# A hybrid trunk layer on one core: past latents turned in the input phase, constant key rows taken from them, and the turned inverses queued behind attention's first query splits

## The chip, the core and the metric

The kernel runs on one core of a Trainium2 chip. The time is the device time of one execution in microseconds (us); a kernel's time is the median of its runs. Engines are called as the profile calls them: PE (TensorE, matrix products), PEld (its weight loads), DVE (VectorE), ACT (ScalarE), POOL (GpSimd) and SP (SyncE, which only issues DMAs here). Each engine works through its own queue of instructions in order.

## The reference

One layer of a streaming encoder for two groups of requests that share the weights: 1024 prompt tokens and 32 sample tokens, which continue streams with 512 past positions. The kernel handles them as T = 1056 columns of an fp32 activation with 1024 features.

```python
x = LN(alpha * x + Mix(x))      # Mix: attention | S5 | RWKV-7, then one output projection
x = LN(alpha * x + MLP(x))      # squared ReLU, hidden 4096

def mla_mixer(q_lat, kv_lat, k_rope_raw, pos, ckv_past, krope_past, prm):
    q = (rms_norm(q_lat, g_q) @ w_qb)          # 6 heads x (64 nope + 32 rope)
    ckv = rms_norm(kv_lat, g_kv); krope = apply_rope(k_rope_raw, cos, sin)
    ckv_all = concat([ckv_past, ckv]); krope_all = concat([krope_past, krope])
    kv = ckv_all @ w_kvb                       # k_nope | v
    return attend(mla_scores(q_nope, q_rope, k_nope, krope_all), v), ckv, krope
```

For the prompt there is no past and the mask is causal in chunks of 64. RWKV-7 is a linear recurrence with a matrix state per head; the kernel works it in chunks of 64, for which it needs the inverse of a 64 x 64 unit triangular matrix per chunk and head.

## The kernel before, in words

The matrix products of the three large projections are made in fp32 accuracy out of three products of split operands (a high part, hi, and the rest, lo: `split3`, hi on ACT in L49, lo on DVE or POOL in L50; `mm3`, L63, L65, L67). Tokens run in blocks of 384, 384 and 288, contracted features in tiles of 128, eight to a block.

The program has four stages. *Input phase* (to about 306 us): the input projection comes in tiles of 128 output columns (PSUM tag "acc", three buffers; weights wmraw, split to wmhi and wmlo). The first of these tiles that matter here give the low-rank part (`lmix`, a column tile whose mixing with the token before, L238 and L239, feeds `stage_lora`: tanh and sigmoid on ACT as lact, L262 to L264; the gate gt, L297 to L305). Then follow the RWKV tiles of three head pairs (`PAIRS`, 2, 1, 0), the key latent ckv, the rope key (`stage_kr`, L150 to L170), the query latent qn and its products (`stage_q`, L1142: products L1159, evictions L1160, loads of wqa, wqr, ropec and ropes in L1165 to L1177, stores to q_d in L1172) and u (`stage_u`). Latents are normalised with L184 to L191: a square on ACT, a sum over partitions on PE (L185), and L186, L90, L91, L191 on DVE with three small ACT steps between.

*Unit inverses.* Each pair's products for the chunk matrices stand in `rwkv_m` (L718: L726 on PE, evicted at L730; the sample's 32 x 32 block p8 per head, L732 and L733, with the PSUM tag "pti", one buffer; stores to mt_d at L738). `rwkv_inv` (L743) loads all of them as 108 x 2 blocks of 32 x 32 (nn, L755) and inverts them by 31 steps on DVE (L760 product, L761 sum), one after the other. The result y is copied turned (zt, L764, on ACT) and both are stored (zt_d L765, xt_d L766, SP) and loaded again as zb and zc (L777, L778), on which L788 forms the off-diagonal blocks; the inverses go to xt_d (L794) and from there to the scan.

*Attention beside the scan* (to about 840 us): `side_by_side` (L1295) advances two generators, step 0 for attention and S5 and step 1 for the inverses' end and the RWKV scan, with leads of 10 and 14 steps and then 2.5 steps of attention to one of the scan. A scheduler puts the instructions in each engine's order by priorities; `high_priority` lifts a part, and `issue_after` forbids a part to be queued ahead of a given instruction. Step 1 is lifted by 120, and at the first turn must follow the last SP instruction traced so far. Attention itself begins with `attn_past` (L1068: loads of the 512 past latents and rope keys, eight transposes into PSUM, cpast L1079 and kpast L1086), then `attn_setup` (L1089). That makes three key buffers kh, kl and two query buffers qh, ql with a constant row at partition 96 (-1, the rows up to 127 zero), which carries the row maximum through the score product. The constant rows are written into kr (the loaded rope key, whose buffer is also that of the query loads, tag "q") and kpast by memsets (L1102, L1103), split with them, and subtracted from themselves for the zero query rows (L1111). `attn_keys` (L1114) makes the key products sck and splits them, `attn_q` (L1197) loads a head's query (L1202) and splits it, and `attn_max` forms the first scores (sc, PE, L63 to L67). The scan's products begin with pra (L833), on ld loaded from rw.

*Output projection, MLP and the two layer norms* fill the rest, to 1608 us.

## Time and profile before

| what | value |
|---|---|
| runs of the kernel | 1610.67, 1611.26, 1625.8 us; median 1611.26 |
| profiled execution, its own time | 1609.9 us |
| its span | 1608.1 us |
| mean clock granted to PE | 0.965 of full |
| PE busy | 1487.7 us, 93% |
| DVE, ACT, POOL busy | 920.6, 510.6, 415.9 us |

A timeline row has the start and the length in us, the engine, the line of the kernel, the operation, the tile written <- the tiles read, the shape and a count of like instructions that follow each other; in brackets the idle time of the engine ahead of it and what ended that. SPq and ACTq are DMA issues on these engines' queues. A row of waits has the engine and the tile, the instruction that it waited for, the us in total, how often, and the longest. A row of windows has the stretch and its length, the busy us of PE, PEld, DVE, ACT and POOL with the number of instructions, the granted clock, the share of the DMA engines and GB/s. A row of a group has the number of instructions, their busy time and mean in ns, and the idle time before them.

### The profile page before, as it was taken

What the parts mean: (1) busy time and instruction counts of PE and PEld (TensorE: products, weight loads), DVE (VectorE), ACT (ScalarE), POOL (GpSimd) and SP (SyncE); (2) the same over time, 40 slices, a digit from 0 to 9 for tenths busy, and PEclk for the clock granted to TensorE, in tenths of its full rate; (3) what the DMA queues carried; (4) which work ended last, traced back from release to release, by engine and by line L of the source; (5) the groups of instructions that cost most, each with busy time, mean ns of one, the idle gap of its engine ahead of it and who ended that gap; (6) DMA issues with size and microseconds to landing.
All of it is one profiled execution on the core that took longest, in us unless ns stands there. A gap on an engine that the chain in (4) does not pass through costs nothing. (4 is left out here: it accounts for less than half of the span.)

```text
span 1608.1 us, 26358 instructions
## 1 busy us (share of the span) xinstructions
PE 1487.7 (93%) x10855; PEld 1336.1 (83%) x10855; DVE 920.6 (57%) x1676; ACT 510.6 (32%) x991; POOL 415.9 (26%) x394
## 2 busy tenths in 40 slices
PE   7899898578899798888999999999999999999995
PEld 7889786466667566566879999999999999999995
DVE  8476959363566544453865755554454454545457
ACT  5344433314544545542323212222121112221122
POOL 4623663511121101211422221222121112221123
PEclk9999999788999999999999999999999999999998
DMA  5314471437233221233512111111111111111012
GB/s 183 132 59 175 148 191 31 115 87 127 71 86 87 63 75 42 72 98 92 174 56 79 40 40 41 52 53 49 44 43 50 40 40 53 53 40 53 14 41 82
DMA packets 112621, 123.50 MB, mean 77 GB/s; under 512 B 51280, under 2 KB 87812, under 8 KB 112120
## 3 DMA queue, kind: packets, MB, share of 16 engines
q1 hardware_dynamic: 92516, 102.53, 21.8%
q10 hardware_dynamic: 19632, 18.27, 3.8%
q8 instruction: 85, 1.39, 0.4%
q0 software_dynamic: 352, 1.01, 0.2%
q14 instruction: 36, 0.29, 0.1%
HBM read 89.05 MB, written 32.68 MB: 76 GB/s over the span
## 5 line engine op out<-in xcount | busy, mean ns | idle before, releaser
L63 PE MATMUL acc<-xh,uphi 128*128 128x384 f32 (+1 forms) x768 | 249.0, 324 | 0.0
L65 PE MATMUL acc<-xl,uphi 128*128 128x384 f32 (+1 forms) x768 | 248.1, 323 | 0.0
L67 PE MATMUL acc<-xh,uplo 128*128 128x384 f32 (+1 forms) x768 | 247.8, 323 | 0.0
L1538 DVE TENSOR_TENSOR rl<-rl 128x384 f32<-128x384 f32 (+1 forms) x96 | 142.2, 1481 | 176.2 <-ACT rl L1537 174.3
L1566 DVE TENSOR_TENSOR yacc<-yacc,acc 128x384 f32<-128x384 f32 (+2 forms) x344 | 158.9, 508 | 112.1 <-PE acc L67 112.0
L63 PE MATMUL acc<-hh,dnhi 128*128 128x384 f32 (+2 forms) x736 | 209.3, 320 | 0.0
L65 PE MATMUL acc<-hl,dnhi 128*128 128x384 f32 (+2 forms) x736 | 207.2, 320 | 0.0
L67 PE MATMUL acc<-hh,dnlo 128*128 128x384 f32 (+2 forms) x736 | 197.5, 319 | 0.0
L50 POOL TENSOR_TENSOR dnlo<-dnraw,dnhi 128x1024 fp32r<-128x1024 f32 x30 | 72.5, 2417 | 336.8 <-ACT dnhi L49 321.5
L63 PEld LDWEIGHTS acc<-xh,uphi 128*128 128x128 f32 x768 | 144.2, 188 | 0.2 <-ACT xh L49 0.2
L65 PEld LDWEIGHTS acc<-xl,uphi 128*128 128x128 f32 x768 | 144.3, 188 | 0.0
L67 PEld LDWEIGHTS acc<-xh,uplo 128*128 128x128 f32 x768 | 144.3, 188 | 0.0
L50 POOL TENSOR_TENSOR uplo<-upraw,uphi 128x1024 fp32r<-128x1024 f32 x34 | 81.6, 2401 | 238.3 <-ACT uphi L49 238.3
L63 PE MATMUL acc<-xh,wmhi 128*128 128x384 f32 (+3 forms) x384 | 131.9, 344 | 9.3 <-ACT xh L49 8.2
L65 PE MATMUL acc<-xl,wmhi 128*128 128x384 f32 (+3 forms) x384 | 130.2, 339 | 1.6 <-DVE xl L50 1.6
L63 PEld LDWEIGHTS acc<-hh,dnhi 128*128 128x128 f32 x736 | 131.6, 188 | 0.0
L65 PEld LDWEIGHTS acc<-hl,dnhi 128*128 128x128 f32 x736 | 131.5, 188 | 0.0
L67 PE MATMUL acc<-xh,wmlo 128*128 128x384 f32 (+3 forms) x384 | 129.6, 338 | 0.0
L67 PEld LDWEIGHTS acc<-hh,dnlo 128*128 128x128 f32 x736 | 128.9, 188 | 0.0
L49 ACT ACTIVATE dnhi<-dnraw 128x1024 fp32r<-128x1024 f32 x30 | 31.8, 1060 | 298.9 <-PE acc L65 249.2
L49 ACT ACTIVATE hh<-rl 128x384 fp32r<-128x384 f32 (+1 forms) x96 | 47.9, 499 | 148.7 <-DVE rl L1538 148.7
L63 PEld LDWEIGHTS acc<-xh,wmhi 128*128 128x128 f32 (+1 forms) x384 | 73.9, 192 | 12.8 <-ACT xh L49 8.5
(489 smaller groups left out, 2881.2 us busy)
## 6 DMA issues: line engine op xcount, KB each, us to landing
upraw<-in_w_up SPq DMA_DIRECT2D x32, 512.0 KB
dnraw<-in_w_dn SPq DMA_DIRECT2D x30, 512.0 KB
ld<-rw SPq DMA_DIRECT2D x24, 320.0 KB
wmraw<-in_w_m SPq DMA_DIRECT2D x12, 512.0 KB
wo<-in_w_out SPq DMA_DIRECT2D x8, 512.0 KB
z<-in_xa SPq DMA_DIRECT2D x8, 512.0 KB
out_y<-o SPq DMA_DIRECT2D x8, 512.0 KB
xr<-in_xt SPq DMA_DIRECT2D x8, 384.0 KB
```

The lines of the kernel that those rows point to most:

```text
L49: nc.scalar.activation(out=hi, in_=ps, func=AF.Copy)
L50: (lo_eng or nc.vector).tensor_tensor(out=lo, in0=ps, in1=hi.bitcast(F32), op=ALU.subtract)
L63: nc.tensor.matmul(out=outs[i], lhsT=lh, rhs=rhs[i][0], start=start, stop=False)
L65: nc.tensor.matmul(out=outs[i], lhsT=lh, rhs=rhs[i][1], start=False, stop=False)
L67: nc.tensor.matmul(out=outs[i], lhsT=ll, rhs=rhs[i][0], start=False, stop=stop)
L1538: nc.vector.tensor_tensor(out=r[:, :n], in0=r[:, :n], in1=r[:, :n], op=ALU.mult)
L1566: nc.vector.tensor_tensor(out=y, in0=y, in1=ps[i][:, :n], op=ALU.add)
```

## The change

It has six parts.

1. `attn_past` is called in the input phase, right behind the low-rank tile. The past is loaded on ACT's queue into the buffers "mix" of that phase, turned through the PSUM tag "pt", and cpast and kpast stay in a pool that lives on. The constant rows of kpast are written there.
2. `attn_setup` takes the constant rows of the first key buffer and the zero rows of the queries from a broadcast column of kpast (three kinds of instruction: POOL differences for qh, ql and kl, one ACT copy for kh). The splits of kr and kpast cover partitions 64 to 95 alone, and kr needs no constant rows.
3. `rwkv_m` puts the sample products of both heads into one PSUM tile, at partitions 0 to 31 and 64 to 95, and evicts them together behind both large evictions.
4. wqr and ropes are loaded on SP's queue instead of ACT's.
5. In `side_by_side` the first turn of step 0 is lifted by 1500, and the first turn of step 1 must also follow the last ACT instruction traced so far.
6. gt has one buffer instead of two, and the temporary of the rope key's turned output (ko) uses a "mix" buffer; wkv is loaded at the start of `stage_attn`.

```diff
@@ stage_kr, stage_lora
-    ko = g.p1.tile([P, 9, 32], F32, tag="krt", name="ko", bufs=1)
+    ko = g.rawp.tile([P, 9, 32], F32, tag="mix", name="ko", bufs=2)
-        gt = g.lq.tile([P, WSH], F32, tag="o", name="gt", bufs=2)
+        gt = g.lq.tile([P, WSH], F32, tag="o", name="gt", bufs=1)
@@ rwkv_m
+    p8 = g.pti.tile([P, TS], F32, tag="pti", name="pti")
     for h in range(2):
+        nc.tensor.matmul(out=p8[64 * h:64 * h + TS], lhsT=bt[hsl(h), SOFF:WSH], rhs=at[hsl(h), SOFF:WSH], start=True, stop=True)
         nc.scalar.activation(out=nm[:, 0:8, h], in_=ps[h], func=AF.Copy)
-        p8 = g.pti.tile([P, TS], F32, tag="pti", name="pti")[:TS]
-        nc.tensor.matmul(out=p8, lhsT=bt[hsl(h), SOFF:WSH], rhs=at[hsl(h), SOFF:WSH], start=True, stop=True)
-        nc.scalar.activation(out=nm[:TS, 8, h, :TS], in_=p8, func=AF.Copy)
+    for h in range(2):
+        nc.scalar.activation(out=nm[:TS, 8, h, :TS], in_=p8[64 * h:64 * h + TS], func=AF.Copy)
@@ attn_past
-    g.wkv = g.ap0.tile([P, 2, 384], F32, tag="wkv", name="wkv")
-    nc.sync.dma_start(out=g.wkv, in_=g.a["w_kvb"])
-    g.cpast = g.ap0.tile([P, 512], F32, tag="cpast", name="cpast")
-    ct = g.ap.tile([P, 4, P], F32, tag="rec", name="ct", bufs=1)
-    nc.sync.dma_start(out=ct, in_=g.a["ckv0"].rearrange("(t p) c -> p t c", p=P))
-    ps = g.psc.tile([P, 4, P], F32, tag="sc", name="sct")
+    g.cpast = g.keep.tile([P, 512], F32, tag="cpast", name="cpast")
+    ct = g.rawp.tile([P, 4, P], F32, tag="mix", name="ct", bufs=2)
+    nc.scalar.dma_start(out=ct, in_=g.a["ckv0"].rearrange("(t p) c -> p t c", p=P))
+    ps = g.pt.tile([P, 4, P], F32, tag="pt", name="pt")
...
+    nc.gpsimd.memset(g.kpast[96:128], 0.0)
+    nc.gpsimd.memset(g.kpast[96:97], -1.0)
@@ attn_setup
+    cz = bc(g.kpast[96:128, 0:1], [32, 1568])
+    for x in g.q2[0]:
+        nc.gpsimd.tensor_tensor(out=x[96:128], in0=cz[:, 0:T], in1=cz[:, 0:T], op=ALU.subtract)
+    nc.scalar.activation(out=g.kh[0][96:128], in_=cz, func=AF.Copy)
+    nc.gpsimd.tensor_tensor(out=g.kl[0][96:128], in0=cz, in1=cz, op=ALU.subtract)
     nc.sync.dma_start(out=kr[64:96], in_=g.kr_d)
-    for x in (kr, g.kpast):
-        nc.gpsimd.memset(x[96:128], 0.0)
-        nc.gpsimd.memset(x[96:97], -1.0)
     for x, o, c, n in ((g.kpast, TP, 0, 512), (kr, 0, 0, TP), (kr, 1536, TP, TS)):
-        split3(g, x[64:128, c:c + n], g.kh[0][64:128, o:o + n], g.kl[0][64:128, o:o + n])
+        split3(g, x[64:96, c:c + n], g.kh[0][64:96, o:o + n], g.kl[0][64:96, o:o + n])
...
-        for x in g.q2[i] if i < 2 else ():
-            nc.gpsimd.tensor_tensor(out=x[96:128], in0=kr[96:128, 0:T], in1=kr[96:128, 0:T], op=ALU.subtract)
+        for x in g.q2[i] if i == 1 else ():
+            nc.gpsimd.tensor_tensor(out=x[96:128], in0=cz[:, 0:T], in1=cz[:, 0:T], op=ALU.subtract)
@@ stage_q
-            nc.scalar.dma_start(out=wr[:, k, j, x:x + 32 * n] ...
+            nc.sync.dma_start(out=wr[:, k, j, x:x + 32 * n] ...
-        nc.scalar.dma_start(out=sn[32 * h:32 * h + 32], in_=g.a["rope"][32:64])
+        nc.sync.dma_start(out=sn[32 * h:32 * h + 32], in_=g.a["rope"][32:64])
@@ side_by_side
-            step(0, a)
+            with g.tc.high_priority(FRONT) if k == 0 else nullcontext():
+                step(0, a)
             n -= 1
         if not done[1]:
-            with g.tc.high_priority(PRIO), g.tc.issue_after(last_traced(g, mybir.EngineType.SP)) if k == 0 else nullcontext():
+            with ExitStack() as s:
+                s.enter_context(g.tc.high_priority(PRIO))
+                for e in (mybir.EngineType.SP, mybir.EngineType.Activation) if k == 0 else ():
+                    s.enter_context(g.tc.issue_after(last_traced(g, e)))
                 step(1, b)
@@ stage_attn
-    attn_past(g)
-    yield
+    g.wkv = g.ap0.tile([P, 2, 384], F32, tag="wkv", name="wkv")
+    nc.sync.dma_start(out=g.wkv, in_=g.a["w_kvb"])
     attn_setup(g)
@@ tile_trunk
                 g.lmix = mixed(g, raw_in(g, 3, 9, w=w0), 9)
+                attn_past(g)
```

The scheduler moves more than these lines say. Line numbers in the changed kernel are one higher from L735 on and three higher behind the set-up. The first place is ACT's queue in the input phase, between the evictions of the third and the fourth column tile. Before:

```order
28 L226 ACTIVATE raw<-acc 128x384
29 L49 ACTIVATE wmhi<-wmraw 128x1024
30 L227 ACTIVATE raw<-acc 128x256
31 L228 ACTIVATE raw<-acc 128x32
32 L262 ACT_TABLE_LOAD
33 L262 ACTIVATE lact<-mix 32x1058
34 L263 ACTIVATE lact<-mix 32x1058
35 L264 ACT_TABLE_LOAD
36 L264 ACTIVATE lact<-mix 64x1058
```

In the change:

```order
28 L1074 DMA ct<-in_ckv 128x4x128
29 L226 ACTIVATE raw<-acc 128x384
30 L1078 ACTIVATE cpast<-pt 128x512
31 L1080 DMA kt<-in_kr 128x4x32
32 L262 ACT_TABLE_LOAD
33 L262 ACTIVATE lact<-mix 32x1058
34 L263 ACTIVATE lact<-mix 32x1058
35 L264 ACT_TABLE_LOAD
36 L264 ACTIVATE lact<-mix 64x1058
37 L49 ACTIVATE wmhi<-wmraw 128x1024
38 L227 ACTIVATE raw<-acc 128x256
39 L228 ACTIVATE raw<-acc 128x32
```

The past's loads and first eviction came in, and the weight split (L49) and two evictions (L227, L228) moved from ahead of the low-rank activations to behind them.

The second place is DVE's queue at the norm of the query latents (L186, L90, L91, L191), which shares the queue with the steps of the inverse (L760, L761; L761, L762 in the change). The last extent of a step's product falls from 512 in its middle to 62 at its end. Before, about step 16:

```order
301 L186 TENSOR_SCALAR pt<-pt 128x384
302 L760 TENSOR_TENSOR tmp<-y,nn 108x512
303 L761 TENSOR_TENSOR y<-y,tmp 108x2x16x16
304 L760 TENSOR_TENSOR tmp<-y,nn 108x510
305 L90 SCALAR_TENSOR_TENSOR rms<-rms,pt 128x384
306 L761 TENSOR_TENSOR y<-y,tmp 108x2x17x15
307 L186 TENSOR_SCALAR pt<-pt 128x384
308 L91 SCALAR_TENSOR_TENSOR rms<-rms 128x384
309 L760 TENSOR_TENSOR tmp<-y,nn 108x504
310 L191 SCALAR_TENSOR_TENSOR qn<-qn,vec,rms 128x384 x2
```

In the change, about step 29:

```order
329 L186 TENSOR_SCALAR pt<-pt 128x384
330 L762 TENSOR_TENSOR y<-y,tmp 108x2x29x3
331 L90 SCALAR_TENSOR_TENSOR rms<-rms,pt 128x384
332 L761 TENSOR_TENSOR tmp<-y,nn 108x120
333 L91 SCALAR_TENSOR_TENSOR rms<-rms 128x384
334 L762 TENSOR_TENSOR y<-y,tmp 108x2x30x2
335 L191 SCALAR_TENSOR_TENSOR qn<-qn,vec,rms 128x384 x2
336 L761 TENSOR_TENSOR tmp<-y,nn 108x62
337 L90 SCALAR_TENSOR_TENSOR rms<-rms,pt 128x384
338 L762 TENSOR_TENSOR y<-y,tmp 108x2x31
339 L91 SCALAR_TENSOR_TENSOR rms<-rms 128x384
```

The norm of the first query block moved from the chain's middle to its last steps (its own first L186 stands behind the 27th product), and the chain's first steps now follow directly on the products of the last head pair, ahead of the key latent's norm.

The third place is ACT's queue about the turned inverse, zt. Before:

```order
248 L1172 DMA q_d<-qnope 64x1056 x2
249 L1160 ACTIVATE qropeb<-scq 128x288
250 L1160 ACTIVATE qropeb<-scq 128x384
251 L764 ACTIVATE zt<-y 108x1024
252 L1160 ACTIVATE qnope<-scq 128x384 x3
253 L148 ACTIVATE ut<-acc 128x8x48 x2
```

In the change:

```order
263 L49 ACTIVATE kh<-sck 64x512
264 L49 ACTIVATE kh<-sck 64x32
265 L49 ACTIVATE qh<-q 96x544
266 L49 ACTIVATE qh<-q 96x512
267 L765 ACTIVATE zt<-y 108x1024
268 L49 ACTIVATE qh<-q 96x512
```

It moved from among the evictions of the query products to behind the splits of head 0's query.

12 lines of the change are left out of this document (6 added, 6 removed).

## The prediction

> **What bounds the kernel now.** I read the page first, then stretches of the span, then what TensorE (PE) waited for, then the rows around each wait.
>
> ```profile
> span 1608.1 us, 26358 instructions
> PE 1487.7 (93%) x10855; PEld 1336.1 (83%) x10855; DVE 920.6 (57%) x1676; ACT 510.6 (32%) x991; POOL 415.9 (26%) x394
> ```
>
> PE is busy for 93% of the span, so time can only come out of its gaps, which lie in the first half. Stretches, with the busy time of PE, PEld, DVE, ACT and POOL, the granted clock, the DMA share and GB/s:
>
> ```profile
> 80.00:170.00 90.00, 90.00 (x542) 80.08 (x540) 62.65 (x164) 39.26 (x65) 29.03 (x47) 0.98 0.31 108
> ...
> 280.00:290.00 10.00, 0.51 (x3) 0.05 (x1) 8.02 (x10) 1.64 (x1) 9.46 (x10) 0.69 0.30 76
> ...
> 306.00:322.00 16.00, 6.24 (x20) 2.62 (x18) 8.79 (x11) 7.48 (x15) 15.21 (x12) 0.76 0.44 129
> 322.00:330.00 8.00, 6.00 (x20) 4.60 (x21) 5.94 (x13) 1.23 (x3) 1.72 (x2) 0.62 0.95 230
> ```
>
> From 80 to 170 us PE has no gap at all: work that comes late before 80 is passed on, not absorbed. At 280 to 290 it does half a microsecond of work, and at 306 to 322 six of sixteen. The waits of PE name the causes:
>
> ```profile
> PE scq L1159 <- ACT qnope L1160: 10.2, 1, 10.2
> PE sck L1119 <- DVE kl L50: 9.8, 4, 4.9
> ...
> PE pti L732 <- ACT kk L733: 5.6, 3, 3.3
> ...
> PE scq L1159 <- DVE qn L191: 3.3, 3, 1.6
> ```
>
> The largest one, in a row of ACT and one of PE:
>
> ```profile
> 288.36 1.94 ACT L764 ACTIVATE zt<-y 108x1024 f32<-108x1024 f32 x1 [12.17 <-DVE y L761]
> ...
> 290.73 4.10 PE L1159 MATMUL scq<-qn,wqa 128*128 128x288 f32 x8 [10.23 <-ACT qnope L1160]
> ```
>
> ACT runs its queue in order. The turned inverse (zt) stands between two evictions of query products and waits 12.17 us for the inverse's last step on DVE, at 288; PE finds no free PSUM and stands for 10.23.
>
> **The change, part by part.**
>
> *zt behind head 0's query splits.* The 10.23 us wait goes, and the evictions behind zt run at PE's pace. zt itself is not needed there: its store (L765, row below) went out only at 318.24. That is a gain of 10.2, if nothing else holds the query products.
>
> *The inverse chain and the query norm.* Something else does. The 31 steps of the chain (L760, L761) share DVE with the norms of the key and query latents.
>
> ```profile
> 209.60 0.31 ACTq L738 DMA_DIRECT2D mt_d<-kk  x1
> 215.22 0.34 ACTq L755 DMA_DIRECT2D nn<-mt_d  x1
> 218.62 2.44 POOL L162 TENSOR_TENSOR krt<-krc,ropek 32x1056 f32<-32x1056 f32 x1
> ...
> 227.07 0.56 DVE L90 SCALAR_TENSOR_TENSOR rms<-rms,pt 128x384 f32<-128x384 f32 x1 [6.37 <-DMA ropec<-in_rope]
> 227.54 0.22 DVE L760 TENSOR_TENSOR tmp<-y,nn 108x62 f32<-108x62 f32 x1
> 251.80 0.56 DVE L186 TENSOR_SCALAR pt<-pt 128x384 f32<-128x384 f32 x1
> 257.58 1.56 PE L1159 MATMUL scq<-qn,wqr 128*128 128x384 f32 x4 [1.31 <-DVE qn L191]
> ...
> 269.90 2.67 POOL L1181 TENSOR_TENSOR qrope<-qrope,ropec 128x1056 f32<-128x1056 f32 x1 [25.53 <-ACT qrope L1160]
> ...
> 270.32 2.62 DVE L761 TENSOR_TENSOR y<-y,tmp 108x350 f32<-108x350 f32 x1
> ```
>
> Before, the chain stood behind a key norm (L90) that waited 6.37 us on ACT, where eight loads of wqr were being issued (the row names the ropec load, the last event by time); it began at 227.54, and the first query norm (L186, 251.80) stood in its middle, 5.8 us ahead of the first query product. In the new order nothing but the loads of nn stands ahead of the chain, and the first query norm stands behind its 27th step. With wqr and ropes on SP, ACT is free of that blockade.
>
> When does the chain begin? Its last input was issued at 215.22, 5.6 us after the last store of the blocks (209.60) that it reads. The pair of sample products spares some of the 5.6 us of pti waits on that path. Bounds: 210 (all of the pti wait off, and 0.5 us to land) and 221 (nothing spared, landing another 5.6 us). I take 214. How long to step 27? The group rows of the two lines:
>
> ```profile
> L761 DVE TENSOR_TENSOR y<-y,tmp 108x62 f32<-108x62 f32 (+15 forms) x31 | 26.9, 868 | 0.8
> L760 DVE TENSOR_TENSOR tmp<-y,nn 108x62 f32<-108x62 f32 (+15 forms) x31 | 22.6, 728 | 0.7
> ```
>
> These 49.5 us hold eight operations like that of 270.32: it took 2.62 beside a POOL product of 2.67, where its neighbours of the same width take about 0.5, some 2.1 us extra each. So the chain's own work is 49.5 - 8 x 2.1 = 33, of which 30 precede the query norm. To it come three key norms (four operations each, like that of 251.80, about 0.5: 6), one mix (twice a norm's operation by its width: 1.3), and six POOL products of 2.4 us like that of 218.62, which now run beside the chain (rope of the key, weight splits, a mix): 6 x 2.1 = 13. Sum 50.3; with the small gaps between steps I use 52, which puts L186 at 266, and with the 4.7 that the norm takes with its interleaved steps, the first query product starts near 270.7 instead of 257.58: **+13.1** (bounds +7 and +22: 210 with one hold fewer at the low end, 221 with one more at the high end). PE arrives earlier than that (by its row it stood free 1.31 ahead of 257.58, at 256.3; at most 3.3 of lateness from below come to it), so it waits there.
>
> [...]
>
> *Query products.*
>
> ```profile
> 294.38 0.63 PE L63 MATMUL acc<-xh,wmhi 128*128 128x384 f32 x1
> ...
> 306.17 0.29 PE L67 MATMUL acc<-xh,wmlo 128*128 128x288 f32 x1
> ...
> 308.02 1.13 PE L1119 MATMUL sck<-ckv,wkv 128*128 128x512 f32 x2 [0.68 <-ACT cpast L1079]
> ```
>
> From 257.58 to the last input block at 294.4 were 36.8 us; less 10.2, and less the rest of the waits on qn (3.3 less the first 1.3, 1.9), leaves 24.7. New: 270.7 + 24.7 = 295.4. The block itself (12.0) and a pair of latent products that now stands inside it (1.1) give 308.5, against 306.4: **+2.1**.
>
> *Attention's set-up.*
>
> ```profile
> 310.56 2.92 POOL L1111 TENSOR_TENSOR ql<-kr 32x1056 fp32r<-32x1056 f32 x1
> ...
> 315.91 1.94 POOL L1111 TENSOR_TENSOR ql<-kr 32x1056 fp32r<-32x1056 f32 x1
> ...
> 317.88 0.32 SPq L1202 DMA_DIRECT2D q<-q_d  x1
> 318.24 0.40 SPq L765 DMA_DIRECT2D zt_d<-zt  x1
> ...
> 322.36 0.45 PE L63 MATMUL sc<-kh,qh 128*128 128x128 f32 x1 [3.33 <-POOL kl L1109]
> ```
>
> From the last input product (306.17 + 0.29) to the first score was 15.9 us. The query load waited for POOL's last constant row at 317.85 to give back kr's buffer. Now kr is read by the splits alone, so the load is free earlier, and turning the past (eight transposes, two evictions, the wait of 0.68 above) is gone from here. Of sck's waits on DVE's splits (9.8 above) the first pair's moves into the last block, ahead of its end. What remains is POOL: the constant rows still stand behind a memset that waited for PE; qh and ql of head 0 (1.94 + 2.92) and kl, 1568 wide, by the same rate 2.92 to 4.3: 7.9 to 9.2 after the last product. I take 9 (bounds 8, and 16 if the set-up stays as it was): **-6.9**. First score at 317.5 instead of 322.36: **-4.8**.
>
> *Early phase.* The eight transposes move to 30 to 50 us.
>
> ```profile
> 37.53 1.06 ACT L49 ACTIVATE wmhi<-wmraw 128x1024 fp32r<-128x1024 f32 x1 [2.62 <-PE acc L65]
> ...
> 45.16 1.09 ACT L262 ACTIVATE lact<-mix 32x1058 f32<-32x1058 f32 x1 [4.91 <-DVE mix L239]
> ...
> 50.31 0.44 PE L63 MATMUL acc<-xh,wmhi 128*128 128x384 f32 x1 [1.11 <-ACT raw L225]
> ```
>
> There the next weight split and two evictions, on ACT from 37.53 before, now stand behind the three lact operations and a table load, the first of which waited until 45.16 for DVE. The eviction behind that group let PE go at 50.31; less its own half microsecond the group ends at 49.8, and with 1.06 and two short evictions (0.6) those are done at 51.5. PE's block of 50.31 needs that split and POOL's behind it (some 2.4), so it starts about 4 later; I estimate that one of them is caught up: 3.3 late at 80 us, and no gap until 170 to absorb it. It costs nothing of its own, because PE arrives at the query products with 8 us to spare; without that cover it costs 3.3 (bounds 0 and 4.2). The p8 pair saves up to 5.6, hidden by the same wait; without that wait it counts.
>
> *Rest.* Three rows on the two smaller edits: who waited for the gate's store, the last load of the inverse's blocks, and the products on them.
>
> ```profile
>   POOL gt L298: 1.6, 1
> ...
> L778 SPq DMA_DIRECT2D zb<-xt_d x4: 427/488/488, 326.1 to 327.7; - x4
> ...
> L788 PE MATMUL pti<-zb,n x128: 191/191/212, 337.9 to 340.5; 32*32 32x32 f32 x128
> ```
>
> One gt buffer instead of two makes POOL wait for that store twice instead of once, at 120 to 135, hidden while PE has blocks in hand (bounds 0 and 2 x 1.6). zt now follows head 0's query splits: its store comes about 1.5 us after the first score instead of 4.1 ahead, 5.6 later. The loads behind it were issued by 327.7; if they land within the 5.6 that the chain's loads had at most, 4.6 us are left to 337.9. So 1 us may be lost: I take 0, bounds 0 and 3. Behind 340 us the order on PE is nearly the same, so the gain there passes to the end.
>
> Sum: +13.1 - 10.2 - 1.9 + 1.1 - 6.9 = -4.8; a colder array after shorter gaps is priced next.
>
> ```profile
> 326.55 0.63 PE L63 MATMUL sc<-kh,qh 128*128 128x512 f32 x1
> ...
> 328.42 0.39 PE L67 MATMUL sc<-kh,ql 128*128 128x512 f32 x1
> ```
>
> After the long gap a 512-wide score took 0.63, then 0.39. A gap of 9 instead of 16 us may start warmer; I take 0.3 off (bounds 0 and 2). [...]
>
> So -5.1: the span goes from 1608.1 to 1603.0, the profiled run (1609.9) to 1604.8. The median shown, 1611.26, stands 1.4 above that run: **1606.2**.
>
> **The rivals.**
>
> *B, the waits simply go.* The chain is through before PE arrives: it starts at 210, and POOL holds it less. Then 10.2, 1.9, the pti waits of 5.6 and the set-up's 6.9 all count, less 1.1 moved and the early 3.3: -20.2, so 1591. For it: 13 us of lead over 227.54. Against it: the query norm's place behind step 27 and the POOL products.
>
> *C, the query norm decides.* The chain starts at 221, with two more holds (4.2): L186 at 277.2, first query product 281.9, first score 328.7, +6.3, and the store of the inverse 2 more: 1620. If the set-up also stays at 16, 1627. Each us of delay counts in full; slower than before begins at a chain start of 219. For it: one row of 5.6 us for such a store-and-load. Against it: DVE waits for nothing else there.
>
> *D, nothing comes through.* The first score comes earlier, but the scan behind it is bound by the inverse and its stores, which do not: 1611. For it:
>
> ```profile
> PE pra L833 <- DMA ld<-rw: 6.7, 2, 6.5
> ```
>
> This wait of 6.5 us at 366 hangs on SP's queue behind the inverse's stores. Against it: those follow L788, which moves with the scores.
>
> **How the numbers follow.** Forecast 0.48 (own range 1598 to 1613), B 0.22, C 0.20, D 0.10. About 1% (16 us) is what a measurement of this kernel can tell from no change. Faster by more (below 1595): most of B and a tail of the forecast, 0.23. Slower by more (above 1627): the far half of C and mishaps of the early phase, 0.14. Within: 0.63. The range 1590.5 to 1622.5 leaves out somewhat less than half of B and the far part of C.
>
> **What would show it.** Right: no wait of L1159 on qnope; instead one wait of 6 to 12 us of the first L1159 on qn L191, near 262 to 271; the chain's first step at 212 to 219 with several of its early steps at 2.4 us; first score 8 to 11 us after the last input product; PE's fourth block 3 to 4 us late at 50 us. Wrong: a first query product before 262 (then B), or after 278 (C), or a PE gap after 330 us that was not there.

## The result, and the profile after

The changed kernel takes 1620.99 us, the median of 20 runs (1615.93 to 1630.71); the kernel before, beside it, 1612.62 (20 runs, 1608.4 to 1625.8). The ratio is 1.0051, with a 95% interval of 1.0033 to 1.0069: 8 us slower, where 5 us faster was forecast. The time lies just inside the top of the range (1622.5), and within what rival C gave (1620 to 1627).

The first lines of the page after. PE is busy nearly as long (1489.2 us against 1487.7), so the loss is in its gaps:

```profile
span 1616.0 us, 26354 instructions
PE 1489.2 (92%) x10855; PEld 1338.5 (83%) x10855; DVE 914.4 (57%) x1676; ACT 513.6 (32%) x992; POOL 416.1 (26%) x393
```

The waits of PE after (total, times, longest). The 10.2 us of L1159 on qnope are gone, as forecast. Two waits of nearly that size stand at the top in their place, and neither is in the prediction: the key norm's sum of squares (L185), and a product of the scan (L841).

```profile
PE pt L185 <- ACT rms L184: 10.0, 2, 6.2
PE sck L1122 <- DVE kl L50: 9.8, 5, 2.4
PE prt L841 <- ACT wu L884: 8.7, 1, 8.7
...
PE acc L63 <- ACT raw L228: 4.3, 1, 4.3
```

The stretches shown before, and one more, 212 to 220 us (busy time of PE, PEld, DVE, ACT, POOL; clock; DMA share; GB/s):

```profile
80.00:170.00 90.00, 89.88 (x549) 79.69 (x550) 65.89 (x168) 43.23 (x73) 31.75 (x49) 1.00 0.37 133
212.00:220.00 8.00, 1.47 (x6) 1.06 (x7) 2.11 (x8) 1.23 (x4) 1.96 (x2) 0.71 0.76 198
280.00:290.00 10.00, 10.00 (x36) 6.65 (x35) 0.78 (x2) 3.80 (x9) 5.84 (x3) 1.00 0.09 19
306.00:322.00 16.00, 8.80 (x45) 6.89 (x43) 8.07 (x11) 8.47 (x16) 13.16 (x11) 0.76 0.46 134
322.00:330.00 8.00, 5.55 (x18) 4.20 (x18) 4.96 (x10) 2.41 (x2) 1.40 (x1) 0.62 0.65 185
```

The kernel before at 212 to 220:

```profile
212.00:220.00 8.00, 8.00 (x46) 7.74 (x45) 0.00 (x0) 2.57 (x5) 7.92 (x6) 1.00 1.00 252
```

At 280 to 290 PE is now full instead of empty. At 212 to 220 it is the other way round: 1.47 us of work instead of 8.00. The gap has moved 70 us ahead.

The places that the prediction spoke of, on the timeline after (start, length, engine, line):

```profile
217.53 0.23 DVE L761 TENSOR_TENSOR tmp<-y,nn 108x62 f32<-108x62 f32 x1 [19.16 <-DMA rw<-mix]
...
267.98 0.56 DVE L186 TENSOR_SCALAR pt<-pt 128x384 f32<-128x384 f32 x1
...
272.72 1.00 PE L1162 MATMUL scq<-qn,wqr 128*128 128x384 f32 x2 [3.25 <-DVE qn L191]
...
298.54 0.44 PE L63 MATMUL acc<-xh,wmhi 128*128 128x384 f32 x1 [0.29 <-ACT ut L148]
...
311.83 0.29 PE L67 MATMUL acc<-xh,wmlo 128*128 128x288 f32 x1
...
322.62 0.44 PE L63 MATMUL sc<-kh,qh 128*128 128x128 f32 x1 [3.48 <-ACT qh L49]
```

Matched product by product, PE is 13 us later than before at 225 to 245 us and 15 later at the first query product; it is 0.3 later at the first score (322.62 against 322.36), 4 to 5 later at 330 to 345, within 2.5 us either way from 360 to 570, 6 to 8 later behind the gap at 584, and 8.6 later from 840 to the last products. So in this execution the wait that went and the waits that came cancel by the first score, and the loss that lasts is taken at 584. Whether that place is the cause is a question for the runs.

### The profile page after: what moved, and what is told of

It is laid out like the page before. It is cut to its first block, busy times and chain, and to the rows that moved or that the text cites. A ratio compares the mean times of both kernels' runs of the same rounds, so it can differ in the third digit from the quotient of the medians.

```text
span 1616.0 us, 26354 instructions
## 1 busy us (share of the span) xinstructions
PE 1489.2 (92%) x10855; PEld 1338.5 (83%) x10855; DVE 914.4 (57%) x1676; ACT 513.6 (32%) x992; POOL 416.1 (26%) x393
## 5 line engine op out<-in xcount | busy, mean ns | idle before, releaser
L65 PE MATMUL acc<-xl,wmhi 128*128 128x384 f32 (+3 forms) x384 | 133.7, 348 | 1.6 <-DVE xl L50 1.6
L49 ACT ACTIVATE dnhi<-dnraw 128x1024 fp32r<-128x1024 f32 x30 | 31.8, 1060 | 301.2 <-PE acc L65 249.2
L49 ACT ACTIVATE hh<-rl 128x384 fp32r<-128x384 f32 (+1 forms) x96 | 47.9, 499 | 148.8 <-DVE rl L1545 148.8
```

The costliest lines, as they stand in the source:

```text
L49: nc.scalar.activation(out=hi, in_=ps, func=AF.Copy)
L65: nc.tensor.matmul(out=outs[i], lhsT=lh, rhs=rhs[i][1], start=False, stop=False)
```

## Where PE stands at 212 to 238

Rows of ACT, DVE and PE in the changed kernel, in order of time (mt_d and rw are stores, "ACTq" their issue):

```profile
204.28 2.19 ACTq L739 DMA_DIRECT2D mt_d<-kk  x4
206.51 2.06 ACTq L336 DMA_DIRECT2D rw<-mix  x1
...
210.91 0.34 ACTq L336 DMA_DIRECT2D rw<-mix  x1
211.29 0.44 ACTq L337 DMA_DIRECT2D rw<-mix  x1
...
219.04 0.52 ACT L184 ACTIVATE rms<-ckv 128x384 f32<-128x384 f32 x1 [6.77 <-DMA rw<-mix]
219.62 1.65 PE L185 MATMUL pt<-rms,ones 128*128 128x384 f32 x2 [6.21 <-ACT rms L184]
...
223.69 0.55 DVE L186 TENSOR_SCALAR pt<-pt 128x384 f32<-128x384 f32 x1
231.76 0.55 DVE L90 SCALAR_TENSOR_TENSOR rms<-rms,pt 128x384 f32<-128x384 f32 x1
234.44 0.55 DVE L91 SCALAR_TENSOR_TENSOR rms<-rms 128x384 f32<-128x384 f32 x1
235.34 0.61 DVE L191 SCALAR_TENSOR_TENSOR ckv<-ckv,vec,rms 128x384 f32<-128x384 f32 x1
235.99 0.52 ACT L184 ACTIVATE rms<-ckv 128x384 f32<-128x384 f32 x1 [8.65 <-DVE ckv L191]
236.56 1.65 PE L185 MATMUL pt<-rms,ones 128*128 128x384 f32 x2 [3.77 <-ACT rms L184]
```

The same two instructions in the kernel before, and the square in the change without the pair (run f1 below):

```profile
217.72 0.53 ACT L184 ACTIVATE rms<-ckv 128x384 f32<-128x384 f32 x1 [4.05 <-DMA rw<-mix]
219.29 0.81 PE L185 MATMUL pt<-rms,ones 128*128 128x384 f32 x2
...
212.28 0.52 ACT L184 ACTIVATE rms<-ckv 128x384 f32<-128x384 f32 x1 [3.29 <-DMA rw<-mix]
```

The norm's scratch tile (rms, L180) shares two buffers with mix. The first one comes free when the last mix but one is stored. With the pair of sample products all four stores of a head pair's blocks (mt_d) and a load of them (210.49 on ACT's queue) stand ahead of that store; its issue ends at 211.73, and the buffer is back 7.3 us later. Without the pair (f1) three of the four stores stand ahead of it, its issue ends at 208.47, and the buffer is back 3.8 us later. Before, the square of the first key block waited for a mix store too (until 217.72), so against that kernel the buffer is only 1.3 us late, and L185 starts at the same time. But PE then had input products to work on until 219.29 and waited for nothing. In the new order L185 stands ahead of that work: PE has done 870 input products (counted from the start) ahead of it instead of 912. It is not the pair that brings it forward. With the past's move alone (e7) and in the change without the pair (e6, f1) it stands behind 844, with the pair and the loads alone (e8) behind 900. So the past's move takes PE's work away from ahead of L185, and the pair makes the buffer late.

The second wait is the inverse's. The other buffer holds the last mix, which is stored only at 236.05, so the second block needs the first one's buffer. The four norm operations of the first block on DVE, half a microsecond each, take from 223.69 to 235.95, because they now stand among the chain's first steps; so the buffer is back at 235.95. From 205 us to the first query product PE waits 15.3 us in four places (2.06 on krc, 6.21, 3.77, 3.25), before 4.7 (1.06, 2.28, 1.31). And between 205 and 250 us the array runs 17 us at half clock, before 3.4.

## The experiments

Each group of kernels ran beside the kernel before on one chip, and each ratio is to that. The theories: **G**, the place of S5's activation (L683) on ACT costs the time at 584; **I**, the input phase costs it, ahead of the first score; **N**, the query norm's place behind the inverse's 27th step; **Q**, zt's store ahead of head 1's query load on SP; **M**, the mix buffer that comes back late; **V**, the key norm among the inverse's steps; **P**, the pair costs only where it meets the past's move; **K**, the granted clock: time at half clock gives a lead back.

### The activation at 584

After, the activation's table load waits 9.07 us for its input, and the scan's eviction wu (L884) stands behind it:

```profile
584.07 1.28 ACT L683 ACT_TABLE_LOAD   x1 [9.07 <-DMA zt<-z_d]
585.37 1.98 ACT L683 ACTIVATE zt<-zt 128x2128 f32<-128x2128 f32 x1
587.36 1.28 ACT L76 ACT_TABLE_LOAD   x1
588.65 0.87 ACT L884 ACTIVATE wu<-prw 128x512 f32<-128x512 f32 x2
...
589.31 1.12 PE L841 MATMUL prt<-ident,ld 128*128 128x128 f32 x4 [8.69 <-ACT wu L884]
```

Before, four other operations of ACT had gone ahead of it, and it waited 3.35:

```profile
584.76 1.28 ACT L683 ACT_TABLE_LOAD   x1 [3.35 <-DMA zt<-z_d]
```

No line of the diff touches it; the scheduler moved it. The edit holds it back in the changed kernel (e1) and in the one before (e2):

```diff
-    log_exp_table(g, [nc.scalar.activation(out=zt, in_=zt, func=AF.Gelu_apprx_tanh)], False)
     yield
+    with g.tc.issue_after(last_traced(g, mybir.EngineType.Activation)):
+        log_exp_table(g, [nc.scalar.activation(out=zt, in_=zt, func=AF.Gelu_apprx_tanh)], False)
     yield
```

> The changed kernel with one addition: S5's gelu (L683, which needs two table loads and sixteen loads of z) may not be queued on ScalarE ahead of the instruction that was traced last at its step, which puts it behind the evictions of the next scan block. Theory G (the gelu): the whole loss of the changed kernel is the wait of 8.7 us that TensorE has at 589 us, because the gelu stands ahead of wu, ptk, po and r and waits 9.07 us for its loads. Then that wait is gone, and the span falls from 1616.0 to 1605 to 1609. Rival I (the input phase): the loss is made before 340 us (query products 15 us later than before, second scores 4.2 us later) and only shows at the end; then the span stays at 1613 or above.

Measured: 1617.86 us, 1.0031 [1.0016, 1.0045].

> The kernel before with the same addition. Its own gelu holds r<-prt, and TensorE waits 3.8 us for that at 590. Theory G: that wait goes, and the span falls from 1608.1 to 1604 to 1606. Rival I says nothing of it; a rival within G is that the gelu's readers (s5g) then wait instead: no change, 1607 to 1609.

Measured: 1607.5 us, 0.9974 [0.996, 0.9988]. The activation's place costs both kernels about the same, 0.2 to 0.26%. With it held in both, the change is still 0.57% slower (1.0031 against 0.9974). G falls as the cause, although the profile after shows its whole loss there. All kernels below have this edit, except where said.

### The parts of the change, one by one

zt behind head 0's query splits alone, on the kernel before, the activation not held (e3) and held (e5):

```diff
-            with g.tc.high_priority(PRIO), g.tc.issue_after(last_traced(g, mybir.EngineType.SP)) if k == 0 else nullcontext():
+            with ExitStack() as s:
+                s.enter_context(g.tc.high_priority(PRIO))
+                for e in (mybir.EngineType.SP, mybir.EngineType.Activation) if k == 0 else ():
+                    s.enter_context(g.tc.issue_after(last_traced(g, e)))
                 step(1, b)
```

> The kernel before with one part of the change: the first turn of the inverses' step must also follow ScalarE's last traced instruction (no lift of 1500, the past in its old place). The 10.23 us wait of the query products on zt goes, and the query norm stays in the middle of the chain. Rival I and the prediction's own view: first score 8 to 11 us earlier than 322.4, and most of it reaches the end: span 1598 to 1601. Theory G alone: what is won before 340 us is lost again on the way to 570, since all engines meet again at the scan's first load, and only the gelu's place matters (here a few evictions earlier than before): 1605 to 1611.

Measured: 1612.06 us, 1.0008 [0.9983, 1.0033]. The first score starts at 311.64 instead of 322.36, a lead of 10.7. At 400 us 5 of them are left, at 550 none. (The profile is of this kernel's slowest execution, 1626.31.)

> The kernel before with two edits: zt queued behind head 0's query splits (as in the third run) and the gelu held (as in the second, which came to 0.9974 of before, 1607.5 us). In the third run's profile the first score came 12 us earlier than before, the lead was down to 5 at 380 and 0 at 560, and the gelu's other place then cost 8. Theory I (the input phase decides): with the gelu out of the way some of the lead stays, 0.990 to 0.995 of before. Theory K (the clock): PE is granted half clock in spells of 3.4 us or multiples, and denser work brings more of them later, so that the lead is given back: 0.996 to 1.000.

Measured: 1601.79 us, 0.9945 [0.9925, 0.9965], against 0.9974 with the activation held alone. The first query product is at 255.28 and the first score at 307.76. Of 13.5 us of lead (321.28 in e2) some 5 reach the end. This part does what it says.

The past's move, the constant rows and the smaller buffers alone (e7), and the pair of sample products with the loads on SP alone (e8):

> The kernel before with the gelu held and, of the change, only the early past with its constant rows and the smaller buffers (no pair, loads of wqr and ropes on ScalarE, zt where it was, no lift). Theory I: it costs the early wait of 4.3 us at 51 us, which is made good by 100, and the set-up is shorter: 0.993 to 0.998. If the early past itself is what loses (ScalarE's queue at 40 us, or the set-up bound by something else), 1.000 to 1.004.

Measured: 1614.91 us, 1.0013 [0.999, 1.0035].

> The kernel before with the gelu held and, of the change, only the pair of sample products and the loads of wqr and ropes on SyncE. The chain then goes ahead of the key norms, the first query norm behind step 20 or so, and zt stands earlier among the evictions. Theory I: the key norms and the query products wait for the chain, 5 to 9 us, and zt's wait is not removed: 1.000 to 1.005. Theory K: 0.996 to 0.999, as without them.

Measured: 1605.98 us, 0.9964 [0.9943, 0.9986]. Against 0.9974 the past's move costs some 0.4%, and the pair and the loads gain nothing that can be told. In e7 the first query product comes at 264.47, 8.2 us later than in e2 (256.30), without any pair. In e8 PE waits 5.74 us at L185, as in the changed kernel, and yet starts the query products at 256.47; its first score, at 310.56, is 10.7 us earlier than in e2, and no gain from it can be told in the time. All of the change but the past's move and the constant rows (h2):

> The kernel before with the pair of sample products, the loads on SP, zt behind the query splits, and the activation of S5 held back: the change without the past's move and the constant rows. Theory P (TensorE is made late at 200 to 240 us only where the pair meets the past's move): first query product at 256 to 258 us, query products through by 284, first score at 306 to 311, ratio 0.990 to 0.995. If the pair alone makes it late: first query product at 265 or later, ratio 0.999 to 1.003. If the time is set by half-clock spells (theory K), as with zt's move alone: first score as early, and the ratio no better than 0.998.

Measured: 1603.93 us, 0.9956 [0.993, 0.9981]; first query product at 261.4, first score at 315.4. PE does wait there for the key norm, once, 5.53 us, so theory P's "only where they meet" is wrong for the wait. The ratio is that of zt's move alone (e5), though the first score is 7.7 us later.

The whole change without the pair, the activation held (e6) and not held (f1):

```diff
-    p8 = g.pti.tile([P, TS], F32, tag="pti", name="pti")
     for h in range(2):
-        nc.tensor.matmul(out=p8[64 * h:64 * h + TS], lhsT=bt[hsl(h), SOFF:WSH], rhs=at[hsl(h), SOFF:WSH], start=True, stop=True)
         nc.scalar.activation(out=nm[:, 0:8, h], in_=ps[h], func=AF.Copy)
-    for h in range(2):
-        nc.scalar.activation(out=nm[:TS, 8, h, :TS], in_=p8[64 * h:64 * h + TS], func=AF.Copy)
+        p8 = g.pti.tile([P, TS], F32, tag="pti", name="pti")[:TS]
+        nc.tensor.matmul(out=p8, lhsT=bt[hsl(h), SOFF:WSH], rhs=at[hsl(h), SOFF:WSH], start=True, stop=True)
+        nc.scalar.activation(out=nm[:TS, 8, h, :TS], in_=p8, func=AF.Copy)
```

> The changed kernel with the gelu held (1.0031 of before) and without the pair of sample products (each head's again by itself). The order on VectorE is then near that of before: the first query norm stands behind step 20 of the chain, not behind step 27. Theory I: the pair is what lets the chain go first; the first query product comes at 258 to 264 instead of 272.7, and of the 9 us by which the changed kernel lies behind the one before, both with the gelu held, 5 or more go: 0.994 to 0.999. Theory K: the order here does not matter, 1.001 to 1.005.

Measured: 1599.63 us, 0.9935 [0.9913, 0.9958], the fastest of all, faster than both kernels. PE waits for no square at L185; the query products start 8 us earlier than in the changed kernel:

```profile
214.37 0.81 PE L185 MATMUL pt<-rms,ones 128*128 128x384 f32 x2
...
264.57 0.81 PE L1162 MATMUL scq<-qn,wqr 128*128 128x384 f32 x2
...
315.56 0.44 PE L63 MATMUL sc<-kh,qh 128*128 128x128 f32 x1 [3.44 <-ACT qh L49]
```

> The whole change without the pair of sample products, and with the activation of S5 where the scheduler puts it. With that activation held back the same kernel took 0.9935 of the time before, and the whole change 1.0031. If the pair is what turns the change into a loss (theory N, below), this run is faster than before too: 0.994 to 0.997, with the first query product at 263 to 266 us as in the run with the activation held. If the loss needs the activation's place (theory G), it is at 1.000 or above.

Measured: 1608.67 us, 0.998 [0.9959, 1.0002].

```profile
212.86 0.91 PE L185 MATMUL pt<-rms,ones 128*128 128x384 f32 x2 [1.57 <-ACT rms L184]
...
236.47 0.90 PE L208 MATMUL pt<-ident,ckv 128*128 128x128 f32 x3 [6.06 <-DVE rms L90]
```

The first wait is nearly gone; the second has another form, since PE still meets a key norm that stands among the inverse's steps. So the one part that was priced as a hidden saving turns the change into a loss: without it 0.998 instead of 1.0051, with the activation held 0.9935 instead of 1.0031. It does so only beside the past's move: with zt's move and the activation held, the ratio is 0.9945 with neither (e5), 0.9956 with the pair (h2), 0.9935 with the past's move (e6) and 1.0031 with both (e1). The loads on SP are in all of these but e5, and the lift goes with the past's move. So for the time theory P holds.

### What of the pair costs it

The inverse behind the query norm (e4): the chain is held behind the norm's last operation on DVE.

```diff
+    yield
     for s in range(31):
...
         stage_q_in(g)
+        with tc.issue_after(last_traced(g, DVE)):
+            next(inv)
```

> The changed kernel with the gelu held (as in the first of these runs) and with the 31 steps of the inverse put behind the query norms on VectorE. The first query product comes as soon as its latents are there, at 255 to 260 instead of 272.7; the first score at 306 to 312 instead of 322.6. If earlier scores reach the end (rival I turned round), the span is 8 to 14 below that of the first run, 1592 to 1599. If the scan's start sets the pace after 370 us (theory G alone), it is within 3 us of the first run.

Measured: 1621.32 us, 1.0051 [1.0038, 1.0065]. It only moved the wait: the key splits on DVE now stand behind the chain.

```profile
PE sck L1124 <- DVE kl L50: 31.4, 5, 25.7
```

The query norm ahead of the 21st step (f2): the same hold, with the `yield` at `s == 20`.

> The whole change with the activation of S5 held back, and with the query norm ahead of the 21st step of the inverse on VectorE, where the kernel without the pair has it. Theory N says that the pair costs its time through the place of the query norm alone: first query product at 258 to 266 us instead of 273.8, first score at 314 to 318 instead of 323.8, ratio 0.993 to 0.997. Theory Q says that the pair costs it at 330 us, through SP's queue, where zt's store stands ahead of head 1's query load: first score earlier as well, but 4 us or more are given back at 330, ratio 0.998 to 1.001. If neither holds (the time is set behind 340 us, by the clock), 1.003 as without this edit.

Measured: 1615.08 us, 1.0007 [0.9983, 1.0032].

```profile
219.87 1.65 PE L185 MATMUL pt<-rms,ones 128*128 128x384 f32 x2 [6.46 <-ACT rms L184]
236.84 1.65 PE L185 MATMUL pt<-rms,ones 128*128 128x384 f32 x2 [4.30 <-ACT rms L184]
271.58 2.01 PE L1165 MATMUL scq<-qn,wqr 128*128 128x384 f32 x4 [2.36 <-DVE qn L191]
```

The first query product came only 1.9 us earlier than in e1 (273.43). N falls: the norm was late because PE was, and PE was late at L185.

zt's store from ScalarE (f3: `nc.scalar.dma_start(out=g.zt_d, in_=zt)`), and with the norm early as well (f4):

> The whole change with the activation of S5 held back, and zt's store issued from ScalarE, right behind zt, so that head 1's query load does not stand behind it on SP. Theory Q: the 4.2 us at 330 us go, ratio 0.999 to 1.001 against 1.0031 without this edit. Theory N: first query product still at 273 to 274, ratio 1.001 to 1.003, since only those 4 us can go.

Measured: 1611.92 us, 0.9995 [0.9971, 1.0019]. The ratio is theory Q's, the rows are not:

```profile
320.75 0.52 SPq L768 DMA_DIRECT2D xt_d<-y  x1
327.25 0.31 SPq L1206 DMA_DIRECT2D q<-q_d  x1
...
332.61 1.18 ACT L49 ACTIVATE qh<-q 96x512 fp32r<-96x512 f32 x2 [5.64 <-DMA q<-q_d]
```

Head 1's query load is no longer behind the store, and still goes out only 6 us after the row ahead of it; ACT waits 5.64 us for it (6.88 in the changed kernel, 6.77 in the one before). The wait is not the store's, and why this kernel is faster stays open.

> Both edits together, on the whole change with the activation of S5 held back. If N and Q each hold a part of the pair's cost, this is the sum: first query product at 258 to 266 us, no loss at 330, ratio 0.990 to 0.994, at or below the kernel without the pair (0.9935). If N alone counts, it is as with the norm early alone; if neither, 1.003.

Measured: 1610.74 us, 0.9991 [0.9967, 1.0014]: no better than one of them.

The first block of each norm in a buffer of its own (g1; g4 is the change as it is with this line alone, the activation not held):

```diff
-        w = g.rawp.tile([P, 2, 512], F32, tag="mix", name="rms", bufs=2)
+        w = (g.rawp if b else g.p1).tile([P, 2, 512], F32, tag="mix" if b else "kk", name="rms", bufs=2 if b else 3)
```

> The whole change with the activation of S5 held back, and the first block of each norm in a buffer of another pool (kk, free since the head pairs' stores), so that its square does not wait for the mix buffer. Theory M (the mix buffer and what follows from it cost TensorE its place): the wait of 6.2 at 219 us goes, that at 236 shrinks or goes, first query product at 262 to 268 us instead of 273.8, last input product at 302 to 307, ratio 0.994 to 0.998. Theory V (the key norm's place among the inverse's steps on VectorE): the wait at 219 goes but the one at 236 grows by as much, first query product within 2 us of 273.8, ratio 1.002 to 1.004. Theory K (the time is set by half-clock spells and not by these waits): 1.003.

Measured: 1609.56 us, 0.9974 [0.9952, 0.9996].

> The whole change as it is, with the first block of each norm in the other buffer and nothing else. If theory M holds, it is faster than before or equal: 0.996 to 1.000, against 1.0051 for the change. If not, 1.004 to 1.006.

Measured: 1614.42 us, 1.0007 [0.999, 1.0023], against 1.0051 without that line. Rows of g1:

```profile
199.87 0.81 PE L185 MATMUL pt<-rms,ones 128*128 128x384 f32 x2
...
222.09 1.65 PE L185 MATMUL pt<-rms,ones 128*128 128x384 f32 x2 [8.54 <-ACT rms L184]
...
268.68 0.81 PE L1163 MATMUL scq<-qn,wqr 128*128 128x384 f32 x2
```

The first block no longer waits, but the second takes the mix buffer in its place and waits for the same store; the first query product still comes 5 us earlier and does not wait for its norm. The gain was forecast, the shape of the waits was not.

The inverse behind the key norm alone (g2: the hold of e4, placed behind `stage_kv_in`), and with the buffer (g3):

> The whole change with the activation of S5 held back, and the first step of the inverse held behind the last block of the key norm on VectorE. Theory V: the wait at 236 us goes (the one at 219 stays), the inverse starts near 230 and ends near 290, first query product at 262 to 268, ratio 0.996 to 0.999. Theory M: the wait at 219 stays and carries on, first query product at 268 to 273, ratio 1.000 to 1.003. Theory K: 1.003.

Measured: 1613.09 us, 0.9998 [0.9976, 1.0019]. The wait at 236 goes, that at 224 stays (6.58); first query product at 269.6.

> Both edits. Theories M and V each take half of the ten us: no wait of L185 over 2 us, first query product at 256 to 262 us, first score at 308 to 314, ratio 0.991 to 0.995. Theory K: first score as early, but the ratio no better than 0.998, because the half-clock time between 300 and 800 us grows.

Measured: 1612.4 us, 0.9988 [0.9956, 1.002]. The first query product is at 261.12, the first score at 317.50, later than expected (308 to 314), and the time is no better than with the buffer alone. Here theory K came nearest.

The stores of the blocks from SP, so that the mix store is issued earlier on ACT (h1):

```diff
-            nc.scalar.dma_start(out=dst[c], in_=nmv[64 * c + 32 * f:64 * c + 32 * f + 32, :, 32 * f:32 * f + 32])
+            nc.sync.dma_start(out=dst[c], in_=nmv[64 * c + 32 * f:64 * c + 32 * f + 32, :, 32 * f:32 * f + 32])
```

> The whole change with the activation of S5 held back, and the stores of the inverse's blocks (mt_d) issued from SP instead of ScalarE. Theory M (the mix buffer comes back late because its store is queued behind those four stores): the wait of the key norm's square is at most 2 us and ends by 214 instead of 219, TensorE is at most 6 us late at 240 us, first query product at 262 to 267, first score at 313 to 317, ratio 0.994 to 0.998. If the buffer is late for another reason (the transfers themselves are slow there, with the loads of wqr beside them), the wait stays at 5 us or more, and the ratio at 1.002 to 1.004.

Measured: 1606.46 us, 0.9958 [0.9938, 0.9978], 0.73% less than e1.

```profile
216.50 0.52 ACT L184 ACTIVATE rms<-ckv 128x384 f32<-128x384 f32 x1 [5.77 <-DMA rw<-mix]
217.08 0.91 PE L185 MATMUL pt<-rms,ones 128*128 128x384 f32 x2 [2.17 <-ACT rms L184]
...
231.13 1.65 PE L185 MATMUL pt<-rms,ones 128*128 128x384 f32 x2 [3.88 <-ACT rms L184]
...
267.94 0.91 PE L1163 MATMUL scq<-qn,wqr 128*128 128x384 f32 x2
```

The buffer comes back at 216.5 instead of 219, PE's first wait falls from 6.2 to 2.2, and the first query product is 5.5 us ahead of e1's, without a wait for its norm. That speaks for theory M, though the mix store still needs 6.4 us to land. The edit does not change the buffer alone: the scheduler now puts L185 behind 847 input products instead of 870, and the query norm's last operation behind 23 of the chain's products instead of 30; in g1 and g4 it stands behind 22. So these runs don't part the late buffer from the order on DVE.

## Why the prediction was wrong

- **The chain.** Start forecast at 214 (bounds 210 and 221), measured 217.53; the query norm's first step (L186) at 266, measured 267.98. Right within 4 us, and the norm did wait behind the chain's 27th product, 267.62. Six early steps held beside POOL's products were forecast; seven steps took 2.22 to 2.75 us where the chain's other operations of 224 to 512 columns took 0.39 to 0.69, and each of the seven began within 1.2 us of the start of a POOL operation of 2.4 to 3.5 us (219.99 to 255.00). The 0.5 us to land in the lower bound was the author's estimate, and no run shows it: the last load of nn was issued at 210.49, and the first step on it began 7.0 us later.
- **The first query product.** Forecast 270.7, measured 272.72. The number was right and its cause only in part: PE was to arrive at 256 to 260 and wait 11 us and more; it arrived at 269.5 and waited 3.25. That the number came within 2 us is luck. The forecast "6 to 12 us" of waiting is the mark that failed.
- **The failed step** is PE's arrival at the query products: "PE arrives earlier than that", at 256.3 with "at most 3.3 of lateness from below", and with it "it costs nothing of its own, because PE arrives at the query products with 8 us to spare". The waits for the key norm ahead of that place were put at nothing. They measured 10.0 us (6.21 and 3.77), beside 2.06 on krc and 17 us at half clock instead of 3.4, and PE arrived 10 to 13 us later than forecast. The spare time was PE's own work ahead of L185, and the past's move took L185 forward into it: alone, with the smaller buffers, it makes the first query product 8.2 us later (e7 against e2). Of the pair it was written that it "saves up to 5.6, hidden"; what it does to ACT's queue (the block of four stores ahead of the store that frees a buffer) was not looked at, and it adds 8.9 (273.43 in e1 against 264.57 in e6). Runs f1, e6, g4 and h1 take the pair or its consequence away, and each brings the ratio from 1.0031 or 1.0051 down to 1.0007 or less. But f2, f3, f4 and g2, which leave the first wait, also come to between 0.9991 and 1.0007; by the intervals only e6 is clear of all of them. "DVE waits for nothing else there" was true and missed the point: the key norm waits for DVE, and PE for the key norm.
- **Query products and last block.** 24.7 and 13.1 forecast, 25.8 (272.72 to 298.54) and 13.6 (to 312.12) measured. **Set-up**: 9 forecast, 10.5 measured (312.12 to 322.62), since ACT's query split waited 1.27 for its load. The four misses, 2.0, 1.1, 0.5 and 1.5, add up to 5.1: the whole forecast lead of 4.8 at the first score, and 0.3 more. The 0.3 taken off for a warmer start was the author's estimate as well, and no run shows it: the granted clock is 0.50 from 314.4 to 328.1 us in both traces.
- **Early phase.** The wait came, 4.3 us at 51, but the sizes were off: PE was 5.5 us late at 60 (about 4 forecast) and 0.9 at 80 (3.3 forecast). It caught up at 74 to 80, where the array ran at full clock (1.00) and in the kernel before at 0.59, and by 100 nothing was left.
- **zt's store.** Forecast 0 (bounds 0 and 3). The first product on the inverse's blocks comes 19.5 us after the first score (342.2) instead of 15.5: 4 us, outside the bounds, and made up by 380.
- **"Behind 340 us the order on PE is nearly the same, so the gain there passes to the end"** is the second step that failed. Of the 13 us between the forecast change of the span (-5.1) and the measured one (+7.9), 5.1 arise by the first score and the rest behind it, with a PE gap of 8.69 us at 584 to 589, where the kernel before had one of 3.78; the prediction names such a gap as a sign of being wrong. e3 lost 11 us of lead by 550, and in e5 5 of 13.5 us reached the end. The order on PE is the same there, but the order on ACT is not (the activation at 584), and PE's clock is not. The pair shows it with the activation held: e1 is 7.9 us behind e6 at the first score and 19 from 410 on. From 320 to 360 us e1's granted clock is 0.63 and e6's 0.88, so some 30 and 10 us at half clock; by an estimate that gives 10 of the 11 us in these two executions. Other executions need not fall so.
- **Rival C** gave the time (1620) from another mechanism: its chain start (221) and its first query product (281.9) did not come.

What stays open: not all of the 8 us has a place. Of each microsecond gained at the first score only a part shows at the end, differently from kernel to kernel; the edits of f2, f3 and g1 gain 0.2 to 0.6% each and do not add up (f4, g3). Why the two late waits cost time beside the past's move, and a wait of the same size at L185 in e8 and h2 none that can be told, is not shown.

## What to carry to other kernels

A part that shortens one engine's queue by a few evictions can reorder the DMAs on that queue; ask which of them frees a buffer, who waits for that buffer, and whether PE still has work ahead of the instruction that needs it (here 870 input products ahead of it instead of the 912 of the kernel before, and a buffer back 7.3 us behind its store's issue instead of the 3.8 of f1). Spare time on PE belonged to an order here, not to an interval: it can't be taken over into a new order without reading where the waiting instruction now stands. A part that costs nothing alone can cost beside another one, so take each out of the whole as well as putting it in alone. When the largest new wait in one profile explains the whole loss, hold it back in both kernels before believing it.

## What the hardware showed that was not expected

PE's granted clock in the 20 traces is full or half, nothing between, in stretches that are multiples of 3.41 us. In the kernel before, for one, it is half at 225.69 for 3.41 us, at 184.72 for 6.83 and at 314.43 for 13.65. At half clock the two L185 products of 384 columns took 1.65 us (219.62 after), at full clock 0.81 (219.29 before). I divided each trace into windows of 3.41 us, up to 1580 us, and counted what followed by PE's busy share in a window at full clock: under 40% busy, the next window ran at half clock in 196 of 196 cases; at 40 to 55%, in 79 of 147; above 55%, in 39 of some 8000. A window at half clock was followed by another one in all 254 cases under 80% busy. In the traces before and after alone these are 21 of 21, 6 of 14, 4 of 819 and 25 of 25. So a wait of about 2 us, if it falls into one window, can cost up to 1.7 us more (an estimate: half of 3.41) in each window at half clock that follows, and it matters where the windows lie. In the kernel before, L185's wait of 2.28 us ahead of 225.16 left its window (222.27 to 225.68) 33% busy, and the clock was half from 225.69 to 229.10; L1137's longer one, 2.54 us ahead of 626.55, fell into two windows (621.63 to 628.46), 69% and 56% busy, and the clock stayed full until 672.83.

Most of the scatter goes with this: over 146 of the 147 runs of the kernel before in the five groups of experiments, the 27 with a mean clock of 0.968 or more took 1607.8 us on average, the 24 with 0.960 or less 1618.0, about 10 us per 0.01. The changed kernel's runs had 0.9590 on average, those of the kernel before 0.9641: by that slope, an estimate, 5 of the 9.5 us between their means go with the clock. It can't be told from these runs how much of that is a cause and how much the mark of the waits themselves.
